# One layer of a convolution and SwiGLU trunk: the opening takes the first norm from columns of x, summed on TensorE, instead of from rows

## The chip, the cores and the metric

One core of a Trainium2 chip runs the whole layer in one launch. The metric is the device time of one execution in microseconds (us). The kernel before was timed three times: 1959.57, 1960.4 and 1963.93 us, so its median is 1960.4 us. The engines are called by the profile's names: PE is the matrix engine, PEld its weight loads, DVE the vector engine, ACT the scalar engine, POOL the GpSimd engine, SP the engine that issues most transfers.

## The reference

With one layer, only the gated short convolution and the dense SwiGLU part are left (T = 2048 rows, D = 1024 features, all float32).

```python
def rms_norm(x, g):
    xf = x.astype(jnp.float32)
    y = xf * lax.rsqrt(jnp.mean(xf * xf, axis=-1, keepdims=True) + RMS_EPS)
    return (y * g.astype(jnp.float32)).astype(x.dtype)

def modulate(h, shift, scale):
    return h * (1.0 + scale[:, None, :]) + shift[:, None, :]

def short_conv_mixer(h, w_in, w_conv, w_out):
    bcv = h @ w_in
    gate_b, gate_c, v = jnp.split(bcv, 3, axis=-1)
    u = gate_c * v
    conv = lax.conv_general_dilated(
        u, w_conv[:, None, :].astype(u.dtype),
        window_strides=(1,), padding=[(CONV_WIDTH - 1, 0)],
        dimension_numbers=("NWC", "WIO", "NWC"), feature_group_count=d)
    return (gate_b * conv) @ w_out

def swiglu(h, w_gate_up, w_down):
    g, u = jnp.split(h @ w_gate_up, 2, axis=-1)
    return (jax.nn.silu(g) * u) @ w_down

    c_act = jax.nn.silu(c)
    mod = c_act @ ada_w[i] + ada_b[i]
    sh_m, sc_m, g_m, sh_f, sc_f, g_f = jnp.split(mod, N_ADA, axis=-1)
    h = modulate(rms_norm(x, norm_gains[i, 0]), sh_m, sc_m)
    h = short_conv_mixer(h, conv_w_in[j], conv_w[j], conv_w_out[j])
    x = x + g_m[:, None, :] * rms_norm(h, norm_gains[i, 1])
    h = modulate(rms_norm(x, norm_gains[i, 2]), sh_f, sc_f)
    h = swiglu(h, ffn_w_gate_up[i], ffn_w_down[i])
    return x + g_f[:, None, :] * rms_norm(h, norm_gains[i, 3])
```

The change concerns the first normalised and modulated `h`, for the first 512 rows, and the shift and scale vectors that it needs.

## The kernel before

Everything lies with features on the 128 partitions and rows of x in the free dimension. The rows are worked in two units of 1024, each unit in two halves of 512 rows (CH = 512). The four products run as phases in this order: in0, out0, in1, out1, gu0, down0, gu1, down1 (the digit is the unit). A phase multiplies by a seven-product scheme (P1 to P7) on 2 x 2 blocks of features and rows, so a phase needs its operand tiles and sums and differences of them (A11, A12, A22, S1 to S4). Every float32 operand is split into a rounded high part and a low rest (`h` and `l` tiles, made by ACT and by DVE), and a product costs three fast matmuls: high by high, low weight by high, high by low.

After the opening, the order of work follows tables of slots and due times. The opening, function `start()`, is written out by hand: the order of its lines is the order of the instructions on each engine, since the helper at line 78 records every operation in program order. All operations therefore carry line 78 in the profile and are told apart by tile names.

What the opening has to make for the first half of unit 0:

- The factor 1/rms of each of 512 rows. Before, `load_rows(0)` loads these rows of x as they lie in memory (tiles `xr`, four transfers of 512 KB), ACT squares each and sums it along the free dimension (`squares`), DVE adds epsilon (tile `v`), POOL takes the power -0.5 (`root`, tile `r0q`), DVE spreads the factors on a diagonal (`diagonal`, tile `r0d`), PE multiplies the diagonal by a tile of ones so that the factors lie along the free dimension on all partitions (`spread`, bank `r0b`), and ACT copies that to `r0r`.
- The operand tiles: `f.load("a")` and `f.load("b")` load x transposed (features 0 to 511 and 512 to 1023 of the same rows, 1 MB each, tiles `in0a` and `in0b`). `mult` multiplies a 128 x 512 part by `r0r` on DVE. `shift` applies the per-feature scale `mA` and shift `mB` on ACT. `upper` and `lower` make the high and the low part, tiles `in0A11h`, `in0A11l` (from a) and `in0A12h`, `in0A12l` (from b).
- `mA` and `mB` for two of the eight feature blocks at a time (q = 0 to 3). `scales(q, i)` sums rows of `ada` times silu(c) on DVE (custom operation, tile `ms`), `shifts(q)` multiplies a 128 x 8 tile `cact` by `ada` in eight matmuls with one output row (bank `pms`), `turned(q)` has ACT copy that row and PE transpose it, `fold(q)` has DVE put both into `mA` and `mB`.
- The weights: `advance("blocks", n)` loads blocks of `w_in` (256 KB each), `advance("high", n)` casts on ACT, `advance("low", n)` subtracts on DVE (tiles `in0P`, `in1P`, `in2P` and so on by group).

`products(first, ks)` issues the matmuls, `warm(n)` n matmuls of a tile of ones (bank `wb`, 128 x 512) whose result nothing reads. A float32 matmul shows as two MATMUL and two LDWEIGHTS records in the profile. The second half (512 more rows) keeps its row form before and after: `load_rows(1)`, `squares(1, ...)`, tiles `xr`, `r1q`, `r1d`, `r1r`.

Transfers are issued by SP in the order of the loads. At most eight transfers are under way, as each takes one of eight semaphores in turn and the next user of a semaphore waits for it. ACT issues four small ones first: `vt`, the two halves of the row c on all partitions (`c_half`, 256 KB each) and `ident`.

Of the kernel before, what the change touches and what calls it, by code (L numbers as in the profile page):

```python
# [19 lines left out]
KD = D // P  # L20
NF = FF // P
FH = NF // 2
EPS = 1e-6
CH = 512
# [11 lines left out]
NBIG, NWP, NRAW, NTMP, NRB = 17, 7, 16, 10, 2  # L36
# [13 lines left out]
def hybrid_conv_layer(  # L50
# [31 lines left out]
    V, A, PE, G, SP = map(Engine, (nc.vector, nc.scalar, nc.tensor, nc.gpsimd, nc.sync))  # L82
# [4 lines left out]
    bigs, pairs, raws, sb = (ctx.enter_context(tc.tile_pool(name=n, bufs=1)) for n in ("bigs", "pairs", "raws", "sb"))  # L87
# [3 lines left out]
    def big(name, dt=F32):  # L91
        return bigs.tile([P, 4, CH], dt, tag="big", bufs=NBIG, name=name)
# [50 lines left out]
    ident = const.tile([P, P], F32, name="ident")  # L143
# [73 lines left out]
    def root(v, name):  # L217

        q = sb.tile([P, 4], F32, tag="q", bufs=8, name=name + "q")
        G.tensor_tensor(q, v, mhalf, ALU.pow)  # L220
        yield 1
        return q

    def at_once(gen):
        while True:
            try:
                next(gen)
            except StopIteration as e:
                return e.value

    def diagonal(q, name):
        dg = tmp(name + "d")
        for t in range(4):
            V.tensor_scalar(dg[:, t * P : (t + 1) * P], ident, q[:, t : t + 1], None, ALU.mult)
        return dg

    def spread(dg, name):
        ps_ = bank(name + "b")
        PE.matmul(ps_, one, dg[:, :CH], start=True, stop=True)
        rb = sb.tile([P, CH], F32, tag="rb", bufs=NRB, name=name + "r")  # L240
        A.copy(rb, ps_)
        return rb
# [664 lines left out]
    for s in slots:  # L907
        ph = s.ph
# [4 lines left out]
        else:  # L913
            b = of.setdefault((ph.name, s.n), Blocks(ph.kind, s.grp))
# [14 lines left out]
    steps = {"whole": [0, WHOLE], "blocks": [0, BLOCKS], "low": [0, LOW], "high": [0, HIGH], "sums": [0, SUMS]}  # L929
# [3 lines left out]
    def advance(step, to):  # L933
        st = steps[step]
        while st[0] <= to:
            if step in BEFORE:
                advance(BEFORE[step], st[0])
            getattr(order[st[0]], step)()
            st[0] += 1
# [164 lines left out]
    def from_xt(u):  # L1104
        return lambda t, tok, kk: SP.dma_start(t, xt_d[u * 2 + tok, kk].rearrange("p (a b) -> p a b", a=4))

    def start():
        ph = phases[0]
        rb, mods, rows, xr = {}, {}, {}, {}
        f = Features(ph, from_xt(0), rb, 0)  # L1110
        s2 = [sb.tile([P, KD], F32, tag="ms", bufs=4, name=f"ms1_{h}") for h in range(2)]
        two = lambda ap: ap.rearrange("p (a b) -> p a b", a=2)
        pair_of = lambda t, i: t[:, 2 * i : 2 * i + 2, :]

        def load_rows(tok):
            xr[tok] = [big(f"xr{tok}_{i}") for i in range(2)]
            for r in range(4):
                r0 = tok * CH + r * P
                SP.dma_start(pair_of(xr[tok][r // 2], r % 2), two(x[r0 : r0 + P, :]))

        def load_scale(q):

            t = mods[1, q] = big(f"ada1_{q}")
            for i in range(2):
                SP.dma_start(pair_of(t, i), two(ada[0, 2 * q + i]))

        def load_shift(q):

            t = mods[0, q] = big(f"ada0_{q}")
            for i in range(2):  # L1130
                SP.dma_start(pair_of(t, i), two(ada1[2 * q + i]))

        sq = {}

        def squares(tok, rs):
            if tok not in sq:
                sq[tok] = small(4, f"a{tok}")
            for r in rs:
                t = pair_of(xr[tok][r // 2], r % 2)
                A.activation(t, t, AF.Square, scale=1.0 / 32.0, accum_out=col(sq[tok], r))  # L1140

        def factor(tok, meanwhile=lambda: None):
            v = small(4, f"v{tok}")
            V.tensor_scalar(v, sq[tok], EPS, None, ALU.add)
            steps = root(v, f"r{tok}")
            next(steps)
            meanwhile()
            return diagonal(at_once(steps), f"r{tok}")

        def shifts(q):  # L1150
            t = mods[0, q].rearrange("p a b -> p (a b)").rearrange("p (k n) -> p k n", k=KD)
            rows[q] = bank(f"pms{q}")
            for k in range(KD):
                PE.matmul(rows[q][0:1, :256], col(cact, k), t[:, k, :], start=k == 0, stop=k == KD - 1)

        def turned(q):
            columns(rows[q], mods[0, q][:, 0, :], 2)

        def scales(q, i):
            for h in range(2):  # L1160
                t = mods[1, q][:, 2 * i + h, :]
                V.tensor_tensor_reduce(t, t, c_half[h], 1.0, 0.0, ALU.mult, ALU.add, col(s2[h], 2 * q + i))

        def fold(q):
            n = slice(2 * q, 2 * q + 2)
            t = small(2, f"mf{q}")
            V.tensor_tensor(t, s2[0][:, n], s2[1][:, n], ALU.add)
            V.tensor_tensor(t, t, vt[:, VB + KD + n.start : VB + KD + n.stop], ALU.add)
            V.scalar_tensor_tensor(mA[0][:, n], t, 1.0, vt[:, VG + n.start : VG + n.stop], ALU.add, ALU.mult)
            V.tensor_tensor(mB[0][:, n], rows[q][:, :2], vt[:, VB + n.start : VB + n.stop], ALU.add)  # L1170

        def mult(key, k4):
            t = f.t[key][:, k4, :]
            V.tensor_tensor(t, t, rb[f.place[key][0]], ALU.mult)
# [14 lines left out]
        def products(first, ks, ns=range(3)):  # L1189
            for k in ks:  # L1190
                for n in ns:
                    multiply(slots[first + n], (k,), follow=False)
# [6 lines left out]
            now[0] = i  # L1199
            due()  # L1200

        load_rows(0)
        load_scale(0)
        load_shift(0)
        f.load("a")
        advance("blocks", 2)
        load_scale(1)
        load_shift(1)
        advance("blocks", 4)
        f.load("b")  # L1210
        load_scale(2)
        load_shift(2)
        advance("blocks", 7)
# [18 lines left out]
        b = bank("wb")  # L1232

        def warm(n):
            for _ in range(n):
                PE.matmul(b, one, w, start=True, stop=True)

        warm(8)


        squares(0, range(4))
        for h in range(2):
            A.activation(c_half[h], c_half[h], AF.Silu)
        dg = factor(0)
        rb[0] = spread(dg, "r0")
        scales(0, 0)
        scales(0, 1)
        shifts(0)
        advance("high", 0)
        for k in range(3):  # L1250
            mult("a", k)
        turned(0)
        warm(2)
        fold(0)
        mult("a", 3)
        advance("low", 0)
        for k in range(2):
            shift("a", k)
# [3 lines left out]
            advance("low", 1 + k)  # L1262
        products(0, range(2))
        scales(1, 0)
        scales(1, 1)
        shifts(1)
        advance("high", 4)
        advance("low", 4)
        products(3, range(2), range(1))
        turned(1)  # L1270
        fold(1)
        products(4, range(2), range(1))
        split("a", "A11", range(2, 4))
        products(0, range(2, 4))
        for k in range(4):
            mult("b", k)
        shifts(2)
        scales(2, 0)
        scales(2, 1)
# [9 lines left out]
        v = small(4, "v1")  # L1289
        V.tensor_scalar(v, sq[1], EPS, None, ALU.add)  # L1290
        steps = root(v, "r1")
# [8 lines left out]
        dg = at_once(steps)  # L1300
# [3 lines left out]
        dg = diagonal(dg, "r1")  # L1304
# [84 lines left out]
    for ph in phases[1:]:  # L1389
        f = first[ph.name]  # L1390
# [17 lines left out]
        else:  # L1408
            rb = {}
# [15 lines left out]
    def multiply(s, ks=None, follow=True):  # L1425
# [23 lines left out]
        if last and follow:  # L1449
            g.after(op)  # L1450

    start()
    for i, s in enumerate(slots):
        if i < 3 * LEAD + 2 * (EARLY - LEAD):
# [60 lines left out]
```

## Time and profile before

| | |
|---|---|
| median of three runs | 1960.4 us |
| the profiled execution, its own time | 1961.33 us |
| span in its profile | 1959.5 us |
| mean granted PE clock | 0.998 |
| bytes read from HBM | 329.38 MB |
| POOL busy | 343.8 us (18% of the span) |

The span leaves out 1961.33 - 1959.5 = 1.83 us around the program. Times inside the span are given from its start. A row of the timeline gives start, duration, engine, line, operation, the written tile and the tiles read, shapes and count, and in brackets how long the engine had idled before it and what released it. A row of the chain gives start, duration and what ran or was waited for.

### The profile page before, as it was taken

What the parts mean: (1) busy time and instruction counts of PE and PEld (TensorE: products, weight loads), DVE (VectorE), ACT (ScalarE), POOL (GpSimd) and SP (SyncE); (2) the same over time, 40 slices, a digit from 0 to 9 for tenths busy, and PEclk for the clock granted to TensorE, in tenths of its full rate; (3) what the DMA queues carried; (4) which work ended last, traced back from release to release, by engine and by line L of the source; (5) the groups of instructions that cost most, each with busy time, mean ns of one, the idle gap of its engine ahead of it and who ended that gap; (6) DMA issues with size and microseconds to landing.
All of it is one profiled execution on the core that took longest, in us unless ns stands there. A gap on an engine that the chain in (4) does not pass through costs nothing.

```text
span 1959.5 us, 24903 instructions
## 1 busy us (share of the span) xinstructions
PE 1934.8 (99%) x8454; PEld 1570.0 (80%) x8454; DVE 1446.5 (74%) x2069; ACT 899.6 (46%) x1419; POOL 343.8 (18%) x226
## 2 busy tenths in 40 slices
PE   8899999999999999999999999999999999999998
PEld 4678887878878888888888888888888888888886
DVE  4898898977998776997776755587776655665466
ACT  4543457634446743543333454473333333444452
POOL 0012112211221301243341410120100100111011
PEclk9999999999999999999999999999999999999999
DMA  9369979769996764777665977588654332386534
GB/s 390 138 227 373 339 253 349 268 225 371 323 324 216 279 232 149 238 241 244 213 214 183 313 281 269 192 287 279 203 192 140 127 137 97 118 321 226 196 134 133
DMA packets 207632, 462.14 MB, mean 236 GB/s; under 512 B 24465, under 2 KB 39953, under 8 KB 201105
## 3 DMA queue, kind: packets, MB, share of 16 engines
q1 hardware_dynamic: 181584, 406.40, 60.1%
q10 hardware_dynamic: 25920, 54.16, 7.3%
q8 instruction: 66, 1.08, 0.2%
q14 instruction: 62, 0.50, 0.1%
HBM read 329.38 MB, written 131.09 MB: 235 GB/s over the span
## 4 chain that ended last, share of the span: by engine, by line
PE 80%; DVE 8%; DMA 6%; ACT 3%; issue 2%; SPq 0%; ACTq 0%; POOL 0%; DVEq 0%
PE gu1P L78 21%; PE gu0P L78 18%; PE in0P L78 11%; PE down0P L78 11%; PE down1P L78 11%; PE in1P L78 3%; PE out1P L78 2%; PE out0P L78 2%; DMA x<-xx 1%; PE pms L78 1%; DMA kgu1P<-gu1P 1%; DVE in1b L78 0%; DVE in1y L78 0%; DVE gu0a L78 0%; DMA xr<-x_d 0%
## 5 line engine op out<-in xcount | busy, mean ns | idle before, releaser
L78 DVE TENSOR_TENSOR gu1a<-gu1P,gu1a 128x512 f32<-128x512 f32 x63 | 43.5, 691 | 108.5 <-PE gu1P L78 108.5
L78 DVE TENSOR_TENSOR gu0a<-gu0P,gu0a 128x512 f32<-128x512 f32 x63 | 43.3, 688 | 71.7 <-PE gu0P L78 68.8
L78 POOL TENSOR_TENSOR gu1a<-gu1a 128x512 f32<-128x512 f32 x11 | 19.0, 1731 | 360.0 <-DVE gu1g11s L78 39.9
L78 ACT COPY gu1a<-gu1P 128x512 f32<-128x512 f32 x42 | 24.7, 589 | 96.1 <-PE gu1P L78 85.0
L78 POOL TENSOR_TENSOR nq<-nq,nq 128x512 f32<-128x512 f32 x28 | 42.8, 1529 | 136.1 <-ACT nq L78 131.4
L78 ACT COPY gu0a<-gu0P 128x512 f32<-128x512 f32 x42 | 24.4, 586 | 82.2 <-PE gu0P L78 81.0
L78 DVE CUSTOM_DVE_ANT_0 ada<-ada,c 128x512 f32<-128x512 f32 x80 | 60.1, 762 | 0.0
L78 ACT COPY gu1g<-gu1P 128x512 f32<-128x512 f32 x24 | 14.1, 588 | 92.8 <-PE gu1P L78 88.0
L78 POOL TENSOR_TENSOR gu0a<-gu0a 128x512 f32<-128x512 f32 x11 | 19.4, 1767 | 170.6 <-ACT gu0a L78 45.3
L78 ACT COPY gu0g<-gu0P 128x512 f32<-128x512 f32 x24 | 14.1, 589 | 74.4 <-PE gu0P L78 71.0
L78 POOL TENSOR_TENSOR down0q<-down0q,down0q 128x512 f32<-128x512 f32 x14 | 21.0, 1502 | 148.1 <-ACT down0q L78 148.1
L78 ACT ACTIVATE nq<-xx 128x512 f32<-128x512 f32 x32 | 37.1, 1159 | 17.0 <-DVE xx L78 17.0
L78 POOL TENSOR_TENSOR down1q<-down1q,down1q 128x512 f32<-128x512 f32 x10 | 16.1, 1612 | 148.6 <-ACT down1q L78 148.5
L78 DVE TENSOR_TENSOR gu1g<-gu1P,gu1g 128x512 f32<-128x512 f32 x24 | 16.6, 691 | 24.4 <-ACT gu1g L78 23.0
L78 DVE TENSOR_TENSOR down2P<-down2P,down2P 128x512 fp32r<-128x512 f32 x14 | 11.2, 801 | 29.0 <-ACT down2P L78 29.0
L78 ACT ACTIVATE gu1a<-gu1a 128x512 f32<-128x512 f32 x42 | 26.6, 633 | 13.1 <-DVE xo L78 6.0
L78 ACT ACTIVATE gu0a<-gu0a 128x512 f32<-128x512 f32 x42 | 26.6, 634 | 7.3 <-DVE gu0a L78 6.1
L78 POOL TENSOR_TENSOR out1q<-out1q,out1q 128x512 f32<-128x512 f32 x14 | 19.9, 1422 | 55.2 <-ACT out1q L78 55.1
L78 POOL TENSOR_TENSOR out0q<-out0q,out0q 128x512 f32<-128x512 f32 x14 | 20.8, 1485 | 46.9 <-ACT out0q L78 29.7
L78 DVE TENSOR_TENSOR gu0g<-gu0P,gu0g 128x512 f32<-128x512 f32 x24 | 16.5, 689 | 14.3 <-ACT gu0g L78 12.9
L78 DVE TENSOR_TENSOR xx<-xx,zz 128x512 f32<-128x512 f32 x32 | 25.1, 784 | 1.1
L78 ACT ACTIVATE down0q<-down0z 128x512 f32<-128x512 f32 x16 | 18.4, 1153 | 14.9 <-DVE down0z L78 14.8
(3139 smaller groups left out, 6715.8 us busy)
## 6 DMA issues: line engine op xcount, KB each, us to landing
ada<-ada_d SPq DMA_DIRECT2D x64, 256.0 KB, 5.3
act0A<-gu0a SPq DMA_DIRECT2D x33, 256.0 KB, 3.5
act1A<-gu1a SPq DMA_DIRECT2D x33, 256.0 KB, 2.6
ada<-ada_d SPq DMA_DIRECT2D x16, 512.0 KB, 9.5
zz<-z SPq DMA_DIRECT2D x32, 256.0 KB, 5.7
xx<-xt_d SPq DMA_DIRECT2D x32, 256.0 KB, 5.5
x<-xx ACTq DMA_DIRECT2D x32, 256.0 KB, 5.4
down0S<-act0S SPq DMA_DIRECT2D x8, 1024.0 KB, 7.3
```

The costliest lines, as they stand in the source:

```text
L78: return tc.keep_in_program_order(f(*args, **kwargs))
```

## The change

The first half's rows are no longer loaded as rows. The two column tiles a and b, which the products need anyway, are loaded first, each in two transfers of 512 KB, then the shift and the scale blocks. The squares are made of these columns, half of them on ACT and half on DVE (new tiles `sqa`, `sqb`), those of b are added in pairs on DVE, and 24 matmuls with a moving operand of one column (`mean`, 1/1024 in every place) sum over the features into the bank `r0s`. DVE reduces the six partial sums. The power, the diagonal and the spreading stay, with the spreading done in four matmuls of 128 columns, each after its part of the diagonal. Half of the matmuls of `shifts(0)` and a quarter of `scales(0)` are put ahead of the diagonal. Two of the first eight warming matmuls and one of the later two go. Three of the four `mult("a")` stand behind `fold(0)`, and the four `mult("b")` stand earlier.

```diff
-        def factor(tok, meanwhile=lambda: None):
...
+        def load_columns(key):
+            t, (tok, kk) = big(f"{ph.name}{key}"), f.place[key]
+            f.t[key] = t
+            for i in range(2):
+                SP.dma_start(pair_of(t, i), two(xt_d[tok, kk][:, 2 * i * CH : 2 * (i + 1) * CH]))
+
+        st, sets = bank("r0s"), [0]
+
+        def sums_of(square):
+            for t in range(4):
+                i = 8 * t + sets[0]
+                PE.matmul(st[:, i : i + 1], square[:, t * P : (t + 1) * P], mean, start=True, stop=True)
+            sets[0] += 1
+
+        def squares_of(key):
+            t, to = f.t[key], big(f"sq{key}")
+            for k in range(0, 4, 2):
+                A.activation(to[:, k, :], t[:, k, :], AF.Square)
+                V.tensor_tensor(to[:, k + 1, :], t[:, k + 1, :], t[:, k + 1, :], ALU.mult)
+                yield to[:, k, :], to[:, k + 1, :]
...
-        load_rows(0)
+        load_columns("a")
+        load_columns("b")
+        load_shift(0)
         load_scale(0)
-        load_shift(0)
-        f.load("a")
         advance("blocks", 2)
         load_scale(1)
         load_shift(1)
         advance("blocks", 4)
-        f.load("b")
         load_scale(2)
...
-        warm(8)
-        squares(0, range(4))
+        warm(6)
         for h in range(2):
             A.activation(c_half[h], c_half[h], AF.Silu)
-        dg = factor(0)
-        rb[0] = spread(dg, "r0")
-        scales(0, 0)
+        for both in squares_of("a"):
+            for x2 in both:
+                sums_of(x2)
+        for x2, y2 in squares_of("b"):
+            V.tensor_tensor(x2, x2, y2, ALU.add)
+            sums_of(x2)
+        v = small(4, "v0")
+        V.tensor_reduce(v, st[:, : 4 * 8].rearrange("p (t i) -> p t i", t=4)[:, :, : sets[0]], mybir.AxisListType.X, ALU.add)
+        V.tensor_scalar(v, v, EPS, None, ALU.add)
+        steps = root(v, "r0")
+        next(steps)
+        shifts(0, range(4))
+        scales(0, 0, (0,))
+        q = at_once(steps)
+        dg, b0 = tmp("r0d"), bank("r0b")
+        for t in range(4):
+            c = slice(t * P, (t + 1) * P)
+            V.tensor_scalar(dg[:, c], ident, q[:, t : t + 1], None, ALU.mult)
+            PE.matmul(b0[:, c], one, dg[:, c], start=True, stop=True)
+        rb[0] = sb.tile([P, CH], F32, tag="rb", bufs=NRB, name="r0r")
+        A.copy(rb[0], b0)
+        shifts(0, range(4, KD))
+        scales(0, 0, (1,))
         scales(0, 1)
-        shifts(0)
         advance("high", 0)
-        for k in range(3):
+        mult("a", 0)
+        turned(0)
+        warm(1)
+        fold(0)
+        for k in range(1, 4):
             mult("a", k)
-        turned(0)
-        warm(2)
-        fold(0)
-        mult("a", 3)
         advance("low", 0)
...
         advance("low", 4)
+        for k in range(4):
+            mult("b", k)
         products(3, range(2), range(1))
...
         products(0, range(2, 4))
-        for k in range(4):
-            mult("b", k)
```

How the order on the engines changes is seen at three places. The first is PE from its first matmul to the first product of the layer (`in0P`); before, it reads:

```order
L78 MATMUL wb<-w,one 128x512 x8
L78 MATMUL r0b<-r0d,one 128x512
L78 MATMUL pms_258<-ada_0_150,cact 1x256 x8
L78 MATMUL pms_258<-ident,ada_0_150 128x1 x2
L78 MATMUL wb<-w,one 128x512 x2
L78 MATMUL in0P_0_298<-in0A11h,in0P_267 128x512 x2
```

The same stretch of PE in the changed kernel:

```order
L78 MATMUL wb<-w,one 128x512 x6
L78 MATMUL r0s<-mean,sqa 128x1 x16
L78 MATMUL r0s<-mean,sqb 128x1 x8
L78 MATMUL pms_272<-ada_0_148,cact 1x256 x4
L78 MATMUL r0b<-r0d,one 128x128 x4
L78 MATMUL pms_272<-ada_0_148,cact 1x256 x4
L78 MATMUL pms_272<-ident,ada_0_148 128x1 x2
L78 MATMUL wb<-w,one 128x512
L78 MATMUL in0P_0_327<-in0A11h,in0P_297 128x512 x2
```

The 24 sums stand between the warming and the diagonal, and four of the eight `pms` matmuls have moved ahead of `r0b`. The second place is ACT from its first computation to the first cast of an operand; before:

```order
L78 ACTIVATE cact<-vt 128x8
L78 ACTIVATE xr_0_141,a_234<-xr_0_141 128x1024 x2
L78 ACTIVATE xr_1_142,a_234<-xr_1_142 128x1024 x2
L78 ACTIVATE c_0_78<-c_0_78 128x512
L78 ACTIVATE c_1_79<-c_1_79 128x512
L78 COPY r0r<-r0b 128x512
```

The same stretch of ACT in the changed kernel:

```order
L78 ACTIVATE cact<-vt 128x8
L78 ACTIVATE c_0_78<-c_0_78 128x512
L78 ACTIVATE c_1_79<-c_1_79 128x512
L78 ACTIVATE sqa<-in0a 128x512 x2
L78 ACTIVATE sqb<-in0b 128x512 x2
L78 COPY r0r<-r0b 128x512
```

The two silu of c, behind the squares before, stand ahead of them now. The third place is DVE around `fold(0)` (tiles `mf`, `mA`, `mB`) up to the low part of the third weight tile; before:

```order
L78 TENSOR_TENSOR in0a<-in0a,r0r 128x512 x3
L78 TENSOR_TENSOR mf_277<-ms_0_139,ms_1_140 128x2
L78 TENSOR_TENSOR mf_277<-mf_277,vt 128x2
L78 SCALAR_TENSOR_TENSOR mA_93<-mf_277,vt 128x2
L78 TENSOR_TENSOR mB_95<-pms_258,vt 128x2
L78 TENSOR_TENSOR in0a<-in0a,r0r 128x512
L78 TENSOR_TENSOR in0P_267<-in0b_155,in0P_267 128x512
L78 TENSOR_TENSOR in0A11l<-in0a,in0A11h 128x512
L78 TENSOR_TENSOR in1P_289<-in1b_157,in1P_289 128x512
L78 TENSOR_TENSOR in0A11l<-in0a,in0A11h 128x512
L78 TENSOR_TENSOR in2P_295<-in2b_159,in2P_295 128x512
```

The same stretch of DVE in the changed kernel:

```order
L78 TENSOR_TENSOR in0a<-in0a,r0r 128x512
L78 TENSOR_TENSOR mf_304<-ms_0_139,ms_1_140 128x2
L78 TENSOR_TENSOR mf_304<-mf_304,vt 128x2
L78 SCALAR_TENSOR_TENSOR mA_93<-mf_304,vt 128x2
L78 TENSOR_TENSOR mB_95<-pms_272,vt 128x2
L78 TENSOR_TENSOR in0a<-in0a,r0r 128x512 x3
L78 TENSOR_TENSOR in0P_297<-in0b_154,in0P_297 128x512
L78 TENSOR_TENSOR in0A11l<-in0a,in0A11h 128x512
L78 TENSOR_TENSOR in1P_318<-in1b_156,in1P_318 128x512
L78 TENSOR_TENSOR in0A11l<-in0a,in0A11h 128x512
L78 TENSOR_TENSOR in2P_324<-in2b_158,in2P_324 128x512
```

Two multiplications of `in0a` have moved from ahead of `mB` to behind it.

More of the change, by code (lines that the diff above doesn't have):

```diff
@@ L1140, in squares, with shifts @@
                 A.activation(t, t, AF.Square, scale=1.0 / 32.0, accum_out=col(sq[tok], r))
-        def factor(tok, meanwhile=lambda: None):
[L1143 to L1150, printed above, removed]
+        def load_columns(key):
[15 more added lines that the diff above has]
+                yield to[:, k, :], to[:, k + 1, :]
+        def shifts(q, ks=range(KD)):
             t = mods[0, q].rearrange("p a b -> p (a b)").rearrange("p (k n) -> p k n", k=KD)
-            rows[q] = bank(f"pms{q}")
-            for k in range(KD):
+            if q not in rows:
+                rows[q] = bank(f"pms{q}")
+            for k in ks:
                 PE.matmul(rows[q][0:1, :256], col(cact, k), t[:, k, :], start=k == 0, stop=k == KD - 1)
@@ L1157, in turned, with scales @@
             columns(rows[q], mods[0, q][:, 0, :], 2)
-        def scales(q, i):
-            for h in range(2):
+        def scales(q, i, hs=range(2)):
+            for h in hs:
                 t = mods[1, q][:, 2 * i + h, :]
```

## The prediction

> **What bounds the kernel now.** I read the page first, then the chain of waits for the first 110 us, then the timeline and the stretches of that window. The page gives the span and the chain's shares by engine:
>
> ```profile
> span 1959.5 us, 24903 instructions
> ...
> PE 80%; DVE 8%; DMA 6%; ACT 3%; issue 2%; SPq 0%; ACTq 0%; POOL 0%; DVEq 0%
> ```
>
> Nearly all of the span is matmul work that the change doesn't touch. So the question is only by how much the opening shifts all that stands behind it. The chain in order of time shows what sets the pace there:
>
> ```profile
> 2.12 8.52 DMA xr<-x_d
> ...
> 10.66 1.16 ACT xr L78 x2
> ...
> 12.09 1.04 POOL r0q L78
> ...
> 15.70 4.71 PE pms L78 x16
> ...
> 21.23 0.17 DVE mB L78
> ...
> 25.43 0.70 DVE in2P L78
> ...
> 26.16 2.79 PE in0P L78 x11
> ...
> 40.77 3.56 PE pms L78 x16
> ...
> 46.27 2.10 ACT xr L78 x4
> ...
> 84.94 25.11 PE in0P L78 x88
> ```
>
> The reader is to see four stretches. Up to 10.6 the rows of x land. Up to 26.1 a serial chain runs: squares, power, diagonal, `pms`, `mB`, then the low part of the third weight tile (`in2P`, done at 25.43 + 0.69 = 26.12). From 26.16 to 44.3 the chain lies on PE. From there to 84.9 it alternates between ACT, DVE and PE, in an order that the change leaves alone, and after 84.94 PE is the chain again. Transfers stand in this chain only before 10.6. I therefore ask two things: when does `in2P` get its low part now, and does anything behind it become shorter?
>
> **The serial chain, before and after.** These rows of the timeline carry most of its terms:
>
> ```profile
> 1.17 0.93 ACTq L78 DMA_DIRECT2D c<-c_row_d  x2
> 1.64 10.16 PE L78 MATMUL wb<-w,one 128*128 128x512 f32 x16 [1.64 <-DVE w L78]
> 11.72 1.13 ACT L78 ACTIVATE c<-c 128x512 f32<-128x512 f32 x2
> 13.15 0.88 DVE L78 TENSOR_SCALAR r0d<-ident,r0q 128x128 f32<-128x128 f32 x4 [1.14 <-POOL r0q L78]
> 20.43 0.36 ACT L78 COPY ada<-pms 1x256 f32<-1x256 f32 x1 [1.08 <-PE pms L78]
> 20.85 0.28 PE L78 MATMUL pms<-ident,ada 1*128 1x1 f32 x2 [0.45 <-ACT ada L78]
> 21.43 0.81 ACT L78 ACTIVATE in0a<-in0a,mB,mA 128x512 f32<-128x512 f32 x1 [0.63 <-DVE mB L78]
> 22.27 0.62 ACT L78 CAST in0A11h<-in0a 128x512 fp32r<-128x512 f32 x1
> 28.88 3.62 PE L78 MATMUL pms<-ada,cact 128*1 128x256 f32 x16
> 38.07 2.49 DVE L78 TENSOR_TENSOR in0b<-in0b,r0r 128x512 f32<-128x512 f32 x4
> ```
>
> The same timeline asked from 9 us on has the last seven warming passes alone; the grouped rows of the first 60 us give busy time and mean of DVE's `scales`; and the transfers give the second half of c alone (last number: us from issue to landing):
>
> ```profile
> 8.63 3.17 PE L78 MATMUL wb<-w,one 128*128 128x512 f32 x7
> ...
> L78 DVE CUSTOM_DVE_ANT_0 ada<-ada,c 128x512 f32<-128x512 f32 x16 | 10.2, 688 | 0.0
> ...
> c<-c_row_d ACTq DMA_DIRECT2D x1, 256.0 KB, 7.8
> ```
>
> *Start of the sums.* The columns land as early as the rows did, in four pieces of the same size by 10.6. But ACT now has both silu of c ahead of its first square. The second transfer of c is issued at about 1.65 and lands 7.8 later, at 9.45; its silu takes 1.13 / 2 = 0.57, to 10.05. The first square follows. The end of the kernel has nearest rows for it and for the sums over features:
>
> ```profile
> 1942.31 0.63 ACT L78 ACTIVATE lastq<-down1z 128x512 f32<-128x512 f32 x1 [7.36 <-DVE lastv L78]
> 1942.99 0.97 PEld L78 LDWEIGHTS lasts<-mean,lastq 128*128 128x128 f32 x8 [0.62 <-ACT lastq L78]
> 1943.88 0.30 PEld L78 LDWEIGHTS lastx<-xl,ident 128*128 128x128 f32 x2
> 1944.09 0.16 DVE L78 TENSOR_TENSOR lastv<-lastv,lasts 128x4 f32<-128x4 f32 x1 [1.80 <-PE lasts L78]
> 1945.38 0.88 DVE L78 TENSOR_SCALAR lastd<-ident,lastq 128x128 f32<-128x128 f32 x4 [1.13 <-POOL lastq L78]
> 1945.72 1.16 PE L78 MATMUL lastb<-lastd,one 128*128 128x128 f32 x8
> ```
>
> A square is 0.63, so PE starts its sums at 10.7. Six warming matmuls are over by about 10.0: the old eight ended at 1.64 + 10.16 = 11.8, and the four passes left out took 4 x 3.17 / 7 = 1.8.
>
> *The sums.* A set of four sums is eight passes. From its first weight load to the next work's, that is 1943.88 - 1942.99 = 0.89; I take 0.88. Six sets: 5.3, to 16.0, with some 0.1 for the last to drain. ACT's further squares (about 0.55 each behind one another) and DVE's four squares (2.49 / 4 = 0.62) stay ahead of PE; the last addition of a pair is made at about 13.7. That is also the lower bound: if sums cost nothing, they would still end at 13.7 + 0.9 = 14.6.
>
> *To `r0b` and `mB`.* The reduction of 24 columns has no row; bounds are nothing and one full 128 x 512 operation (0.62). I take 0.16, the row of the small `lastv`, since it is nearest in size; with the addition of epsilon and the hand-over, `v` is ready at 16.4. POOL's power (1.04 in the chain) gives 17.5. The diagonal with its four matmuls: from 1945.38 to 1945.72 + 1.16 = 1.50, to 19.0. Meanwhile PE does half of `pms`, 3.62 / 2 = 1.81, from 16.1 to 17.9, hidden by the power; without that cover it would cost 1.81. The other half: 19.0 to 20.85. Then ACT's copy 0.36, transposes 0.28 and `mB` 0.17, each with its hand-over as in the rows: `mB` ends at **21.8**, against 21.40 before. Of DVE's four `scales` (10.2 / 16 = 0.64 each) one lies beside the power and three behind the diagonal, from 18.4 to 20.3; one multiplication and the three small `mf` and `mA` follow to about 21.5, just ahead of `mB`. `r0r` is there at 19.6.
>
> So 1.16 + 4.71 of the old chain become 5.3 of sums, later by the silu, and half of `pms` comes out of the way. The two nearly cancel: +0.4.
>
> *Behind `mB`.* Before, `in2P` was ready 26.12 - 21.40 = 4.72 behind `mB`. Now DVE has three multiplications of a behind `mB` instead of one: 3 x 0.62, then low, A11l, low, A11l at some 0.61 each, then 0.69: 4.98. ACT's side up to the second A11h (at most 0.81 + 0.62 + 0.62 + 0.81 + 0.62 = 3.5) is done when DVE asks for it at 1.86 + 3 x 0.61 = 3.7. So +0.26, together **+0.65**.
>
> **What the rest of the change is worth.** The first half's rows, 4 x 512 KB, are 2 MB less. At the 419 GB/s of the stretches below that is 5.0 us, by which all loads from the second half's rows on land earlier. Who waits for them?
>
> ```profile
> 34.40 0.16 DVE L78 TENSOR_TENSOR mB<-pms,vt 128x2 f32<-128x2 f32 x1 [4.17 <-PE pms L78]
> 40.90 1.06 ACT L78 ACTIVATE xr<-xr 128x1024 f32<-128x1024 f32 x1 [3.47 <-DMA xr<-x_d]
> 44.35 0.36 ACT L78 COPY ada<-pms 1x256 f32<-1x256 f32 x1 [1.08 <-PE pms L78]
> ```
>
> ACT did, 3.47 us. But then it stood idle again until PE's third `pms` at 44.35, and PE is the chain there. The 3.47 only becomes a longer wait of the same engine: **nothing**. The four `mult("b")` (2.49) move from 38.07 into the 4.17 that DVE waits for PE's second `pms`: nothing. In the old place DVE then starts its `scales` 2.5 earlier, and waits for ACT's casts behind the same 44.35: nothing. The squares on DVE stand where it only waited. Fewer warming matmuls: nothing, as long as the clock holds.
>
> **Sum.** 1959.5 + 0.65 = 1960.15 of span; with the 1.83 outside, 1962.0 for a profiled execution. The profiled run before, 1961.33, lies 0.93 above the median of 1960.4, so I put the forecast at **1961.0**.
>
> **Rivals.** *The clock drops during the sums (slower).* The stretches of one clock window each show busy us of PE, PEld, DVE, ACT, POOL and then the granted clock, DMA share and GB/s:
>
> ```profile
> 11.17:14.58 3.41, 1.12 (x3) 0.30 (x2) 1.60 (x8) 1.68 (x4) 1.02 (x1) 1.00 1.02 417
> 14.58:18.00 3.42, 3.42 (x8) 0.73 (x7) 1.89 (x8) 0.59 (x1) 0.00 (x0) 0.50 1.01 419
> ...
> 69.20:72.60 3.40, 1.38 (x6) 0.60 (x5) 2.80 (x5) 1.66 (x3) 0.00 (x0) 1.00 0.28 113
> 72.60:76.00 3.40, 3.40 (x10) 2.66 (x9) 3.40 (x7) 1.99 (x3) 0.00 (x0) 0.50 1.03 420
> 79.40:82.80 3.40, 2.89 (x11) 1.53 (x9) 2.22 (x4) 2.28 (x4) 0.00 (x0) 1.00 0.00 0
> ```
>
> A window with PE busy for 1.12 or 1.38 of 3.4 us was followed by one at half clock, one with 2.89 was not. The sums fill more than such a window. Whether passes of one column count as busy, no row shows, as all sums before stood among dense matmuls. If they don't, the clock halves at 14.58 (with this execution's window). Then 4.4 sets are done, the other 1.6 take 2.8 instead of 1.4, to 17.4; the first half of `pms` takes 3.62, to 21.0; the clock returns near 21.4, `r0b` ends at 22.2, the second half of `pms` at 24.0, `mB` at 25.0. That is 3.2 behind my sum: 1964.2. With other positions of the window I get 3 to 7 late, 1963.4 to 1967.4. [...] Against: weight loads run without a pause, and the `pms`, which use one output column, ended the slow stretch at 18.00. The point of decision is a busy share between 1.38 and 2.89 in a window. [...]
>
> *The sums are cheaper, or a landing counts (faster).* If sums only follow the last addition, they end 1.4 earlier: 1959.6. If the 5.0 of saved loads reached the chain in full, 1955.4 + 0.65 = 1956; the idle 1.08 at 44.35 speaks against it.
>
> *The change doesn't do what it says:* columns landing early are of no use, since the squares queue behind c. That is part of my forecast; were c early, PE would still be held by ACT's and DVE's squares, with the bound of 14.6.
>
> **How the numbers follow.** Forecast 0.55, with 1959.5 to 1962.5 as its own range from the bounds of the reduction, the sums and the scatter of the runs. Clock rival 0.30. Cheaper sums or landings 0.10. Anything else, mostly later, 0.05. The bound of 0.2%, about what a measurement of this kernel can tell from no change, is 3.9 us: 1956.5 and 1964.3. Slower gets half of the clock rival and part of the rest, 0.18; faster 0.04; within 0.78. The range 1958.5 to 1966.5 leaves out some 0.07 below and 0.08 above.
>
> **What would show it.** Right: the first sum at 10.7 behind ACT's square, six sets in 5.3, `mB` ending near 21.8, `in2P` low near 26.8, the chain from there as before. The clock rival: 0.50 in a window between 11 and 21 and sets of 1.7. Wrong altogether: `mB` before 20.5, or the third `pms` ending before 43, which would mean that PE wasn't the bound of that stretch.

## The result, and the profile after

| | before | after |
|---|---|---|
| median of six runs, us | 1960.28 | 1967.24 |
| lowest to highest, us | 1959.32 to 1963.93 | 1963.7 to 1970.15 |
| the profiled execution, us | 1961.33 | 1967.72 |
| its span, us | 1959.5 | 1965.8 |

The ratio of after to before is 1.0033, with a 95% interval of 1.0023 to 1.0043: the change makes the kernel slower by about 0.33%, beyond the 0.2% of the prediction's bound and beyond the upper end of its range (1966.5).

These lines of the page of the changed kernel answer to the span and the shares of the chain shown of before, and give the bytes read:

```profile
span 1965.8 us, 24999 instructions
...
HBM read 327.28 MB, written 131.09 MB: 233 GB/s over the span
...
PE 89%; DVE 4%; DMA 3%; ACT 2%; issue 1%; SPq 0%; ACTq 0%; POOL 0%; DVEq 0%
```

The 2.1 MB of rows are indeed not read (329.38 MB before), and the span is 6.3 us longer. Where it grew, the chain of the changed kernel in order of time shows (start, us, what):

```profile
1.66 8.18 DMA c<-c_row_d
9.86 0.63 ACT c L78
10.49 0.53 ACT sqa L78
11.06 8.27 PE r0s L78 x48
19.33 3.50 PE pms L78 x8
22.83 1.51 PE r0b L78 x8
24.34 1.83 PE pms L78 x8
...
31.29 0.70 DVE in2P L78
...
46.65 3.56 PE pms L78 x16
...
52.15 2.10 ACT xr L78 x4
...
90.84 19.27 PE in0P L78 x62
```

Read beside the chain of before, the reader sees one jump and then a constant shift. The third `pms` start at 46.65 instead of 40.77, the squares of the second half at 52.15 instead of 46.27, the long PE chain at 90.84 instead of 84.94: 5.9 later each time. So all of that was lost before `in2P`, and 0.4 of the 6.3 somewhere behind.

In that opening, two things stand out. The sums (48 records, 24 matmuls) took 8.27, and the two halves of the same `pms`, eight records each, took 3.50 and 1.83. The stretches at half clock in these profiles last 3.41 us or a multiple of it (14.58 to 18.00 before, 13.44 to 23.68 here, which is 3 x 3.413) and begin whole multiples apart (72.60 - 14.58 is 17 x 3.413 before, 324.05 - 13.44 is 91 x 3.413 here). A window is such a stretch of 3.41 here, whatever its clock. The windows of the opening say why. The columns are window, us, busy us of PE, PEld, DVE, ACT, POOL with instructions, then granted clock, DMA share, GB/s:

```profile
9.88:13.29 3.41, 2.23 (x20) 2.23 (x21) 1.67 (x3) 2.69 (x5) 0.00 (x0) 1.00 1.01 411
13.29:16.70 3.41, 3.41 (x19) 3.41 (x18) 0.77 (x2) 0.00 (x0) 0.00 (x0) 0.52 1.03 411
16.70:20.12 3.42, 3.42 (x16) 2.80 (x16) 0.72 (x3) 0.00 (x0) 0.28 (x1) 0.50 1.03 419
20.12:23.53 3.41, 3.41 (x10) 1.35 (x9) 2.50 (x11) 0.00 (x0) 1.11 (x1) 0.50 1.03 414
23.53:26.94 3.41, 2.96 (x18) 1.53 (x17) 1.52 (x6) 1.47 (x3) 0.00 (x0) 0.98 1.03 423
```

For three windows PE ran at half clock. The stretches shown lie a little early, which the 0.52 and the 0.98 tell: asked in steps of 0.02 us, the clock falls at 13.44 and is back at 23.68. The stretch from 13.29 to 16.70 holds sums and nothing else on PE; its row calls PE busy for all of it, and the next one is at half clock again. The window from 20.12 holds `pms` and `r0b`, and the one behind it is at full clock. That is the prediction's first rival, the clock that drops during the sums.

### The profile page after: what moved, and what is told of

Read it like the earlier page. It is cut to its first block, busy times and chain, and to the rows that moved or that the text cites. A ratio compares the mean times of both kernels' runs of the same rounds, so it can differ in the third digit from the quotient of the medians.

```text
span 1965.8 us, 24999 instructions
## 1 busy us (share of the span) xinstructions
PE 1942.1 (99%) x8502; PEld 1579.7 (80%) x8502; DVE 1451.4 (74%) x2076; ACT 896.8 (46%) x1415; POOL 343.6 (17%) x226
## 3 DMA queue, kind: packets, MB, share of 16 engines
q8 instruction: 66, 1.08, 0.2%
## 4 chain that ended last, share of the span: by engine, by line
PE 89%; DVE 4%; DMA 3%; ACT 2%; issue 1%; SPq 0%; ACTq 0%; POOL 0%; DVEq 0%
PE gu1P L78 21%; PE gu0P L78 20%; PE in0P L78 11%; PE down0P L78 11%; PE down1P L78 11%; PE in1P L78 9%; PE out0P L78 3%; PE out1P L78 2%; PE pms L78 1%; DMA kgu0P<-gu0P 1%; DMA y1S<-in1b1s 0%; PE r0s L78 0%; DMA c<-c_row_d 0%; DMA out0P<-kout0P 0%; DVE gu0c L78 0%
## 5 line engine op out<-in xcount | busy, mean ns | idle before, releaser
L78 DVE TENSOR_TENSOR gu1g<-gu1P,gu1g 128x512 f32<-128x512 f32 x24 | 16.6, 691 | 23.2 <-ACT gu1g L78 21.8
```

What stands on the lines that cost most here:

```text
L78: return tc.keep_in_program_order(f(*args, **kwargs))
```

## The experiments

Two theories were to be told apart. **Theory:** passes with one moving column don't keep the clock, however densely they follow one another. **Rival:** the clock falls for another reason (PE's idle 1.55 us ahead of the sums, two warming matmuls fewer, a later chain), or the time goes into the later start and the moved parts. Ten kernels ran, one of them the changed kernel once more. All ratios are to the kernel before, timed on the same chip; the times of before in the three groups were 1960.23 (33 runs), 1960.12 (32) and 1959.78 (21). The times given are medians; the ratios and their intervals come from all runs and differ a little from the ratio of the medians. Each kernel has one profiled execution, and its time can lie at the edge of that kernel's runs; where it does, the text says so.

**One-column passes put into the kernel before (p_narrow).** They fill PE's idle time ahead of `r0b`; nothing reads what they make.

```diff
         warm(8)
+        for i in range(10):
+            PE.matmul(b[:, i : i + 1], one, mean, start=True, stop=True)
```

> The kernel before, with ten float32 matmuls of one moving column (20 passes, about 2.2 us) in the gap of 2.3 us that PE has between its eighth warming matmul and the spreading of the factors. Nothing reads them. Clock theory (passes of one column don't count as busy): the clock still falls in that stretch, r0b takes about 1.6 and the first pms 4.7, time as before (1960.3, within 0.5). Rival (any matmul stream keeps the clock, and the loss of the change is the work of the sums): the clock stays at 1.00, r0b 1.1 and the first pms 3.6, some 1.6 us less than before.

Measured: 1960.62 (10 runs), ratio 0.9998, interval 0.9989 to 1.0007. Two windows of its profile:

```profile
12.25:15.67 3.42, 1.97 (x9) 0.83 (x9) 2.45 (x9) 1.02 (x3) 0.94 (x1) 0.98 1.04 426
15.67:19.08 3.41, 3.41 (x10) 1.05 (x9) 1.67 (x6) 0.48 (x2) 0.00 (x0) 0.52 1.01 408
```

The half clock of before (14.58 to 18.00 there) is still there; it begins at 15.55, just inside the first stretch shown. That fits the theory but doesn't show it alone: the added passes run from 10.41 to 12.70, so most of them lie in the window before, and 1.97 of busy time may be too little whatever its width.

**Wide passes in the same place (p_wide).** Two more warming matmuls and one of 256 columns, unread as well.

```diff
-        warm(8)
+        warm(10)
+        PE.matmul(b[:, : CH // 2], one, w[:, : CH // 2], start=True, stop=True)
```

> The kernel before, with two and a half more warming matmuls of 512 columns in the same gap (five passes, about 2.15 us). Both theories: the clock stays at 1.00 through the opening, r0b 1.1, first pms 3.6 instead of 4.7, mB about 1.6 earlier, time about 1958.7. If it does not, the drop of the clock is not a matter of PE's gap.

Measured: 1960.77, ratio 1.0002, interval 0.9993 to 1.0011. One window and two lines of its chain:

```profile
13.89:17.30 3.41, 3.06 (x12) 1.11 (x13) 2.74 (x10) 0.59 (x1) 0.00 (x0) 1.00 1.02 426
```
```profile
10.13 8.16 DMA in0a<-xt_d
18.38 1.90 DVE in0a L78 x3
```

The clock was 1.00 through the whole opening of this execution, with PE busy 3.08 of 3.41 us in the window ahead (10.48 to 13.89), where before it was 0.50 behind a window with 1.12. That fits that matmuls with wide moving operands in that gap keep the clock. But the time I had expected to fall stayed: the chain now waits for the columns of x, which land at 18.3, and `mB` starts at 20.66 instead of 21.23, not 1.6 earlier. The half clock of before was partly covered by a load. The profiled execution (1959.25) is the fastest of the ten runs, and the median is not below that of before at all. That expectation of the time was a miss.

**Sums with 128 moving columns in the changed kernel (e_dense).** The same 24 matmuls, each with the tile of ones as moving operand, accumulated in one bank, so that DVE's reduction goes and the mean is taken by a scalar. Weight loads, order and the late start stay.

```diff
-                i = 8 * t + sets[0]
-                PE.matmul(st[:, i : i + 1], square[:, t * P : (t + 1) * P], mean, start=True, stop=True)
+                c = slice(t * P, (t + 1) * P)
+                PE.matmul(st[:, c], square[:, c], one, start=sets[0] == 0, stop=sets[0] == 5, skip_group_check=True)
...
-        V.tensor_reduce(v, st[:, : 4 * 8].rearrange("p (t i) -> p t i", t=4)[:, :, : sets[0]], mybir.AxisListType.X, ALU.add)
-        V.tensor_scalar(v, v, EPS, None, ALU.add)
+        V.tensor_scalar(v, st.rearrange("p (t n) -> p t n", t=4)[:, :, 0], 1.0 / D, EPS, ALU.mult, ALU.add)
```

> The changed kernel with the same 24 sums, each with 128 equal columns (the tile of ones) as moving operand instead of one; they are accumulated over the six sets in one bank, and the reduction of 24 columns falls away. The weight loads, which pace the sums, stay. Clock theory: no 0.50 between 11 and 23 us, a set takes 0.9, six sets end near 16.5, mB ends near 22.3, and the kernel comes down from 1967.2 to about 1961.5. Rival (the sums cost what they cost, or the late start behind the silu of c is the loss): the sums take as long as with one column, or longer, and the time stays at 1967 or above.

Measured: 1961.06 (11 runs), ratio 1.0007, interval 0.9998 to 1.0015. From the windows and the chain of its profile:

```profile
8.99:12.40 3.41, 1.88 (x17) 1.87 (x17) 1.54 (x3) 2.71 (x5) 0.00 (x0) 1.00 1.03 415
12.40:15.80 3.40, 3.40 (x33) 3.40 (x32) 1.13 (x2) 0.00 (x0) 0.00 (x0) 1.00 1.02 411
15.80:19.20 3.40, 3.16 (x20) 1.72 (x18) 2.10 (x8) 0.00 (x0) 1.40 (x1) 1.00 1.05 421
19.20:22.60 3.40, 2.95 (x14) 1.08 (x12) 2.95 (x12) 1.84 (x4) 0.00 (x0) 1.00 1.03 413
22.60:26.02 3.42, 2.15 (x6) 0.84 (x6) 3.42 (x7) 3.36 (x7) 0.00 (x0) 1.00 1.04 420
26.02:29.43 3.41, 3.41 (x9) 2.36 (x10) 3.41 (x11) 1.12 (x3) 0.00 (x0) 0.51 1.03 407
```
```profile
10.53 5.64 PE r0s L78 x48
...
18.21 1.16 PE r0b L78 x8
19.37 1.83 PE pms L78 x8
```

A window filled by sums alone is now followed by full clock. Even the window ahead of it, with only 1.88 us of sums behind PE's idle time, held the clock, where the changed kernel lost it behind 2.38 us of one-column sums (10.03 to 13.44). The sums take 5.64 instead of 8.27, and most of the loss is gone. A second drop appears at 26.08, behind a window with 2.15 busy, in which PE waits for the casts and low parts of the first product. This profiled execution (1964.21) is the slowest of the eleven runs.

**Eight warming matmuls in the changed kernel (after_w8).** The one-column sums stay. They now follow the warming closely, without PE's idle 1.55.

```diff
-        warm(6)
+        warm(8)
```

> The changed kernel with the two left-out warming matmuls put back at the front: eight instead of six, then the sums of one column as they are. They end near 11.8 instead of 10.0, so the sums start at 11.8 instead of 11.06. Theory (passes of one column don't hold the clock): sums fill the time from 11.8 to beyond 17, so a window of 0.50 follows as before, between 13 and 23, the sums take over 7 us, mB starts at 25 to 28, and the time stays near 1966 (1964 to 1968). Rival (the window lost its share because two warming matmuls went): no 0.50 between 11 and 22, sums 5.4 to 5.9, mB near 22.6, time 1961 to 1962.

Measured: 1963.48 (1960.13 to 1967.96, 11 runs), ratio 1.0019, interval 1.0010 to 1.0028. Four windows of its profile:

```profile
9.10:12.50 3.40, 3.40 (x21) 2.29 (x20) 1.59 (x3) 2.71 (x5) 0.00 (x0) 1.00 1.04 420
12.50:15.90 3.40, 3.40 (x33) 3.40 (x32) 1.09 (x2) 0.00 (x0) 0.00 (x0) 1.00 1.02 409
15.90:19.30 3.40, 3.40 (x10) 1.00 (x10) 2.18 (x9) 0.00 (x0) 1.40 (x1) 0.51 1.05 421
19.30:22.70 3.40, 3.17 (x17) 1.56 (x16) 2.57 (x10) 1.30 (x3) 0.00 (x0) 0.99 1.02 410
```

The window from 12.50 to 15.90 is the twin of the one from 12.40 to 15.80 above: 32 and 33 records, weight loads without a pause, full clock, no idle time. What differs is the moving operand, one column against 128, and with it the place of the results: the wide sums are accumulated in one bank, which was not tried by itself. The next window has 0.51 against 1.00. Neither idle time nor the warming can explain that pair: the window ahead was busy throughout here (3.40) and only 1.88 there.

The window of 0.50 came as expected, the rest was a miss. The clock fell only at 15.94, when the sums were nearly done, so they took 5.5 (10.61 to 16.14) and not over 7, one window is slow in this place and not three, `mB` starts at 23.31 and not at 25 to 28, and the median lies below the expected 1964 to 1968. The profile shows one more slow window, from 26.18 to 29.59, behind one with 2.08 busy, as in e_dense. Its own time (1961.38) is among the lowest of the eleven. The runs scatter widely: the two with a mean granted clock of 0.998 took 1961.12 and 1961.38, the two with 0.994 took 1967.22 and 1967.96. One window at half clock takes 3.41 x 0.5 / 1960 = 0.0009 off that mean, so by this estimate the latter two had some four slow windows more; where these lay, no trace shows.

**The silu of c behind the squares (e_silu).** One-column sums again, started earlier.

```diff
-        for h in range(2):
-            A.activation(c_half[h], c_half[h], AF.Silu)
         for both in squares_of("a"):
...
             sums_of(x2)
+        for h in range(2):
+            A.activation(c_half[h], c_half[h], AF.Silu)
```

> The changed kernel with the two silu of c behind the four squares on ACT again. Clock theory: the sums start at about 9.6, behind the warming matmuls, instead of 11.06, so more of them run before the clock falls; it still falls (0.50 for two or three windows); about 2 to 3 us less than the changed kernel, so 1964 to 1965.5. Rival (the queue behind the silu is the loss): 5 us or more less, 1962 or below, with the sums at one speed throughout.

Measured: 1962.97 (10 runs), ratio 1.0012, interval 1.0002 to 1.0021. Its chain and one pair of windows:

```profile
10.00 5.89 PE r0s L78 x48
15.89 3.50 PE pms L78 x8
```
```profile
11.00:14.41 3.41, 3.41 (x33) 3.41 (x32) 1.02 (x2) 1.31 (x3) 0.00 (x0) 1.00 1.02 418
14.41:17.82 3.41, 3.41 (x13) 1.98 (x13) 1.01 (x4) 0.00 (x0) 1.43 (x1) 0.50 1.05 416
```

The earlier start lets most sums end before the clock falls, but a window of sums alone is again followed by half clock, at 14.41, and the first half of `pms` pays for it. So the late silu is not what halves the clock. It is a large part of the price, though: with the earlier start alone the ratio falls from 1.0033 to 1.0012, and an interval that reaches from 1.0002 to 1.0021 can't be told from that of e_dense. The time is a miss for the theory (1964 to 1965.5) as for the rival (1962 or below); the windows decide here, not the time.

**Both together (e_dense_silu).** The two edits above in one kernel.

> The changed kernel with sums of 128 moving columns and with the silu of c behind the squares. Clock theory: no 0.50 between 9 and 23 us, sums start near 9.6 and end near 15, mB ends near 20.8, and the time is 1959 to 1960.5, below the one with the dense sums alone (1961.1). If the start of the sums did not matter once the clock is kept, it stays at 1961.

Measured: 1958.5 (11 runs), ratio 0.9993, interval 0.9984 to 1.0002. From its chain:

```profile
8.78 5.37 PE r0s L78 x48
...
16.36 1.16 PE r0b L78 x8
...
24.46 0.69 DVE in2P L78
```

No window up to 97 us is at half clock in its profile, and `in2P` starts at 24.46, 1.0 ahead of the kernel before. The interval takes in no change, and the median is half a us below the range expected; the profiled execution (1956.49) is the fastest of the eleven. Against e_silu, with the same order and one-column sums, the ratio is 0.9993 instead of 1.0012, each to the kernel before on its own chip, and the two intervals just touch. That difference is the worth of the wide sums when all else stays.

**The other parts alone (p_order).** The kernel before with only the moved multiplications and one warming matmul fewer.

```diff
-        for k in range(3):
-            mult("a", k)
+        mult("a", 0)
         turned(0)
-        warm(2)
+        warm(1)
         fold(0)
-        mult("a", 3)
+        for k in range(1, 4):
+            mult("a", k)
...
         advance("low", 4)
+        for k in range(4):
+            mult("b", k)
...
         products(0, range(2, 4))
-        for k in range(4):
-            mult("b", k)
```

> The kernel before with the remaining parts of the change alone: one warming matmul instead of two ahead of the products, three multiplications of a behind mB instead of one, the four of b earlier. The norm and the loads are those of before. Expected by the prediction's sum: mB as before (21.4) or up to 0.2 earlier, the low part of the third weight tile 0.26 later, time within 0.5 of 1960.3. If the clock falls between 22 and 30 us for want of the second warming matmul, 1 to 1.5 us more.

Measured: 1960.35 (1957.62 to 1963.66, 11 runs), ratio 1.0007, interval 0.9999 to 1.0016. Two windows ahead of the first `pms` behind the products:

```profile
21.91:25.32 3.41, 2.15 (x6) 0.97 (x6) 3.41 (x7) 3.27 (x6) 0.00 (x0) 1.00 1.02 411
25.32:28.70 3.38, 3.38 (x9) 2.27 (x8) 3.38 (x11) 1.23 (x2) 0.00 (x0) 0.51 1.03 430
```

By the interval these parts cost at most 0.16%. In this execution they bring the same second drop as in e_dense, behind a window with the same 2.15 busy; in the profile of before the clock fell only at 14.58 and 72.60, and once more at 1956.77, in its last 3 us. But these parts don't always bring it. The changed kernel has them too, and a window with just as much busy time, and kept its clock behind it:

```profile
27.09:30.51 3.42, 2.15 (x5) 0.69 (x5) 3.42 (x7) 3.25 (x6) 0.00 (x0) 1.00 1.04 408
```

The next window there, up to 33.92, is at 1.00. So the busy time of the window doesn't settle this drop; what does stays open.

**The warming matmul put back (e_dense_w2).** The dense sums with `warm(2)` instead of `warm(1)` ahead of `fold(0)`.

> The dense sums (128 columns) with the one warming matmul put back that the change takes from the two ahead of the first product. Theory (the pair bridges PE's idle time up to the first product, and without one of it the clock can fall between 22 and 30, as it did with the dense sums at 26.02): no 0.50 between 22 and 34, the third pms start near 29.7 instead of 30.97, time 1959.9 (1959.0 to 1960.5). Rival (one pass of 0.4 us is too little to matter, and only the window's position decides): 0.50 there as with the dense sums or not, as it falls, and a time of 1961 within 0.5.

Measured: 1960.34 (11 runs), ratio 1.0003, interval 0.9994 to 1.0011. Its windows in that place:

```profile
21.48:24.90 3.42, 2.96 (x8) 1.25 (x8) 3.04 (x7) 2.72 (x5) 0.00 (x0) 1.00 1.04 417
24.90:28.31 3.41, 3.08 (x12) 1.92 (x12) 3.41 (x9) 2.13 (x4) 0.00 (x0) 1.00 1.02 408
```

No drop there in the profile, and the time lies where the theory put it. But the intervals of e_dense and e_dense_w2 overlap almost wholly, and the changed kernel and e_dense_silu, with `warm(1)`, show no drop there either. So whether this one matmul matters is left open.

The same profile holds a second twin. Its window of wide sums lies almost exactly where e_silu has its window of one-column sums (11.00 to 14.41), again with 33 and 32 records, and the clock stays:

```profile
11.10:14.51 3.41, 3.41 (x33) 3.41 (x32) 1.99 (x3) 0.83 (x2) 0.00 (x0) 1.00 1.03 422
14.51:17.93 3.42, 3.35 (x22) 1.93 (x21) 0.93 (x4) 0.00 (x0) 1.40 (x1) 1.00 1.04 411
```

**The changed kernel once more (after_again).**

> The changed kernel unchanged, on the chip of the other three. Clock theory: 0.50 for two or three windows between 11 and 24 us, six sets of sums in some 8 us, 4 to 7 us above the kernel before on this chip, scattered with where the free windows fall.

Measured: 1965.65 (1962.33 to 1969.84, 11 runs), ratio 1.0030, interval 1.0021 to 1.0039. The loss is there on another chip, 5.5 above the kernel before, as expected; in the chain of this profile the sums read

```profile
10.97 8.60 PE r0s L78 x48
19.56 3.50 PE pms L78 x8
```

**A version from these findings (v3).** Columns as in the change, but squares of a and of b added in pairs (four sets instead of six), sums with 128 moving columns, silu behind the squares, `warm(2)`, and two casts and low parts of weights placed earlier around `fold(0)`, with two multiplications of a behind them. Its core:

```diff
         warm(6)
+        n = 0
+        for key in ("a", "b"):
+            for x2, y2 in squares_of(key):
+                V.tensor_tensor(x2, x2, y2, ALU.add)
+                for t in range(4):
+                    c = slice(t * P, (t + 1) * P)
+                    PE.matmul(st[:, c], x2[:, c], one, start=n == 0, stop=n == 3, skip_group_check=True)
+                n += 1
...
-        advance("high", 0)
+        advance("high", 1)
         mult("a", 0)
         turned(0)
-        warm(1)
+        advance("high", 2)
+        warm(2)
         fold(0)
```

> A version made from what the first four runs showed: columns as in the changed kernel, squares added in pairs for both tiles (four sets of sums instead of six), sums with 128 moving columns, the silu of c behind the squares, casts of the weight tiles and their low parts ahead of the second low part of a, two warming matmuls kept ahead of the products. If the clock and the serial chain are what costs: clock 1.00 up to 26 us, sums end near 13.8, mB ends near 19.9, the first 18 products are done near 25.7 instead of 28.9, and the time is about 3 us below the kernel before, 1957. If the part behind 44 us is bound by something that the shift does not reach, such as the rows of the second half landing, the gain stays under 1 us.

Measured: 1955.78 (1953.1 to 1957.1, 10 runs), ratio 0.9977, interval 0.9968 to 0.9986: faster than both kernels. From its chain:

```profile
12.10 1.16 PE r0s L78 x8
13.26 1.82 PE pms L78 x8
15.08 1.09 PE r0b L78 x8
...
25.44 3.55 PE pms L78 x16
```

The sums end at 13.26 and the first `pms` behind the products start at 25.4 instead of 28.9. The gain is 4.3, more than the 3 expected. Its parts were not timed one by one, so their shares stay open.

## Why the prediction was wrong

**The step that failed is the choice of the forecast: that PE's clock holds while the sums run** ("Fewer warming matmuls: nothing, as long as the clock holds", with 0.55 for the case and 0.30 for the rival). I had weighed against the rival that weight loads run without a pause and that `pms` had ended a slow stretch. The twin windows (e_dense against after_w8, e_dense_w2 against e_silu) show the first to be no protection: PEld was busy 3.40 of 3.40 us in after_w8, and the next window had 0.51. The second was read off a window that held `r0b` beside `pms` (14.58 to 18.00, PE busy 3.42), and here too the slow stretch ended behind a window with both (20.27 to 23.68, PE busy 3.41). But `pms` has one output row and 256 moving columns; the sums have one moving column. I carried it over from the one to the other.

**What it cost, by the prediction's terms.** From the forecast end of `mB` at 21.8 to the measured one, 27.00 + 0.16 = 27.16 by this row of the timeline:

```profile
27.00 0.16 DVE L78 TENSOR_TENSOR mB<-pms,vt 128x2 f32<-128x2 f32 x1 [0.85 <-PE pms L78]
```

- Start of the sums: 11.06 against 10.7, so +0.4. The second half of c landed at 1.66 + 8.18 = 9.84 and not at 9.45; the order (silu, square, sum) was right.
- The sums: 8.27 against 5.3, so +3.0. Even at full clock six sets are 5.64 (e_dense), not 5.3.
- From the end of the sums to the end of `r0b`: 24.34 - 19.33 = 5.0 against 19.0 - 16.0 = 3.0, so +2.0. At half clock the first half of `pms` takes 3.50 instead of 1.81 and no longer fits beside the power, and `r0b` takes 1.51. This is the case for which the prediction had noted what `pms` costs without its cover.
- Second half of `pms` and the hand-overs to `mB`: 27.16 - 24.34 = 2.8, as forecast.

Together 5.4. **The rival itself was mis-sized as well.** Worked out with the window of before, it gave 3.2 behind the forecast, with `mB` ending at 25.0, and 3 to 7 late with other positions, up to 1967.4. These two are not counted from the same time: 1967.4 is 7 above the kernel before (1960.4), and 7 above the forecast would be 1968.0. Yet the range ended at 1966.5. That the window can lie elsewhere was an assumption there; the runs with one-column sums then showed the first fall between 12.97 and 15.94. The clock fell at 13.44 here, 1.1 earlier than I had put it, and three windows were slow and not two. With a price of 3 to 7 and a chance of 0.30, the range had to reach the upper end of that price. The point of decision between 1.38 and 2.89 of busy time was an estimate from two rows, and no run shows such a point: the profile of before itself has a window with 2.29 (82.85 to 86.26) that full clock followed, 2.15 was followed by half clock in e_dense and by full clock in the changed kernel, and the clock fell behind sums of 2.38 and even of 3.41.

**What held.** From 27.16 to the end of `in2P`, 31.29 + 0.70, are 4.83 against 4.72 before: the three multiplications behind `mB` cost 0.1 where I had 0.26. The saved loads were worth nothing, for the reason given; the row of ACT's third copy now reads

```profile
50.23 0.36 ACT L78 COPY ada<-pms 1x256 f32<-1x256 f32 x1 [4.84 <-PE pms L78]
```

ACT no longer waits for rows of x, and waits 4.84 for PE's third `pms` instead of 1.08. The moved `mult("b")` left no wait in the chain. The longer power (1.40 instead of 1.04 on POOL) was hidden by `pms`.

**What the prediction left out.** With dense sums, where the clock holds during the sums as I had assumed, the kernel is at a ratio of 1.0007 and not clearly different from before, and `mB` ends at 22.03 + 0.16 = 22.2 against the 21.8 of the forecast: its arithmetic was nearly right under its own condition. It had no term for another drop, at about 26, which e_dense, after_w8 and p_order show and the changed kernel doesn't. And the 0.4 behind the opening coincides in the profile of after with one more window at half clock, from 324.05 to 327.47; whether the change has anything to do with that was not tried.

## What to carry to other kernels

Don't read "PE busy 100%" as "the clock will hold": ask how many moving columns the passes have (behind a window of one-column sums the clock was 0.51 and 0.50 here, behind one of sums with 128 columns 1.00; nothing between was tried), and give a reduction over partitions a wide moving operand where it stands outside dense matmuls. The moving operand of 128 equal columns cost no time here against one column: 33 records filled 3.40 us with either, and PEld was busy 3.40 of 3.40. Where a case of the clock is among the rivals, price it over all positions of the window and let the range reach that price.

## What the runs showed of the hardware

- Four windows with weight loads without a pause, PE busy throughout and 33 records each: with 128 moving columns the next window had clock 1.00 (e_dense, e_dense_w2), with one column 0.51 and 0.50 (after_w8, e_silu). The busy time of PE in the profile was 3.40 or 3.41 in all four.
- At full clock the 48 records of the sums took 5.64 with 128 columns (e_dense); with one column 33 records filled 3.40 (after_w8), as many as with 128 (e_dense). At half clock 19 fell into the stretch from 13.29 to 16.70 (clock 0.52) of the changed kernel.
- No single share of busy time separates the two outcomes here. Windows with 2.15 us of PE busy out of 3.41 were followed by half clock in e_dense and p_order and by full clock in the changed kernel (27.09 to 30.51); 1.88 of sums with 128 columns kept the clock (e_dense, 8.99 to 12.40), and 2.38 with one column lost it (the changed kernel, 10.03 to 13.44).
- The place of the fall differs from one execution to the next: with one-column sums the clock first fell at 13.44 and 12.97 (the changed kernel, twice), 14.41 (e_silu) and 15.94 (after_w8). In after_w8 it left the sums nearly untouched (5.5), in the changed kernel it stretched them to 8.27. How much of the scatter between runs comes from this was not measured.
